# Down projection of an encoder layer: another way to form one set of weight sums, a later residual bias, spread convolution taps and another order of the last rows

## The chip, the cores and the metric

The kernel runs on one core of a Trainium2 chip. The metric is the device time of one execution in microseconds (us); the time before is a median of three runs. Beside the times there is one profiled execution, whose trace gives every duration used here. In the trace TensorE is PE (its weight loads PEld), VectorE is DVE, ScalarE is ACT, GpSimd is POOL and SyncE is SP.

## The reference, cut to what matters

One encoder layer on x of 1024 positions by 1024 channels: LayerNorm, a Fourier mixer, LayerNorm, a gated MLP with a depthwise convolution over positions, LayerNorm. All of it is float32.

```
h = layer_norm(DEEPNORM_ALPHA * h + mix, ln_tok_g, ln_tok_b)
u = depthwise_conv(h @ w_up, conv_w, conv_b)       # 2 x 2816 channels, 3 taps
g, v = split(u, 2)
ffn = (silu(g) * v) @ w_down                        # 2816 -> 1024
out = layer_norm(DEEPNORM_ALPHA * h + ffn, ln_ffn_g, ln_ffn_b)
```

The change touches the last stretch: the convolution of the last channel block, the down projection, the residual `ALPHA * h` and the last LayerNorm.

## The kernel before, in words

**Stages.** The mixer and the up projection run first (to 605 us of the span). The up projection goes by 22 channel blocks j of 128 channels; each block leaves a gate half and a value half of 128 channels by 1024 positions. `conv_taps(j, v, part)` starts the convolution of one half with an ACT operation and adds its taps on DVE (line 1086): parts 0 and 1 are two taps of 512 elements, parts 2 and 3 two taps of about 510 and two of one element. `conv_done(j)` applies Silu on ACT (L1120) and multiplies the halves on POOL (L1121); `store(j)` writes the product to the HBM scratch `gd` from ACT's DMA queue.

**Down projection.** It is a 2 by 2 block product done with seven instead of eight sub-products (a Strassen scheme), s = 0 to 6. Each sub-product multiplies a sum of quarters of the activations `g(k, h)` with a sum of quarters of the weights `w(k, h)`, and is 2816/2 channels deep: NK = 11 blocks of 128, taken two at a time as b = 0 to 5 (b = 5 has one). A pair (s, b) is called a block below. Float32 precision comes from splitting each operand into a high and a low part (`split`: ACT writes the high part, L184, DVE the low part, L181), and three matmuls for each product (`mm3`: L190 low x high, L192 high x low, L194 high x high). A full block has 24 matmuls of 512 columns on four PSUM banks `dn`; s = 6 is done row block by row block in the banks `dl`, at the very end.

**How operands are formed.** Three resident sets of tiles are used again and again: `sst[b]` (trace name sa), `tst[b]` (sb), and tiles fetched for one use (qa of activations, qw of weights). A sum is formed by an accumulating DMA from POOL's queue (`pile`, L1135): it adds a quarter from HBM (or from SBUF) onto a tile in place. A minus sign is made by `negate` on ACT (L1138) before the pile. In product 1 the activations are g(0,1) + g(1,1) and the weights w(0,1) - w(0,0): tst is negated and w(0,1) is piled on. Product 3 shows the other way: w(0,0) is fetched into a tile, and DVE subtracts (L1197). Product 2 negates sst and tst again and piles g(0,0) and w(1,1).

**The order of the work.** PE, DVE, ACT and POOL execute in the order in which the program is written, SP's fetches too. In the main loop, n counts the blocks: before block n's matmuls the program issues `down_load` for blocks up to n+5, `down_pile` up to n+4 and `down_prep` (the split) up to n+2. After the matmuls comes `extra(s, b)` with the other work: the last convolution, the loading of the eight accumulators `acc[i]` (the normed h, 128 rows by 1024), their scaling to ALPHA * h (`residual2`: one multiplication by `tokg`, L1220, and one addition of `tokb`, L1221, both on DVE, for each row block and each half), and `down_out(s)`, which adds the banks of a finished product to the accumulators (L1345). Buffers come from one pool of 46 tiles of 4 KB per partition; a fetch or a split waits until the tile whose place it takes has been read for the last time.

**The end.** After block (5, 5) DVE adds the last banks to rows 4 to 7 (L1424), takes the mean and variance (bn_stats, L1365; bn_aggr, L1369), POOL computes the reciprocal root (L223), DVE scales in two steps (L1305, L1314), and SP writes out. Rows 0 to 3 follow as the banks `dl` of product 6 become ready (L1435, L1436). Rows 0 to 3 get the bn_stats of their upper half early, in `extra(5, 2)`. The last row, 3, is written in three pieces: two on DVE, and one on ACT (L1311) and POOL (L1312).

Of the kernel before, what the change touches and what calls it, by code (L numbers as in the profile page):

```python
# [12 lines left out]
AF = mybir.ActivationFunctionType  # L13
ALU = mybir.AluOpType
# [8 lines left out]
NF = DFF // P  # L23
# [129 lines left out]
def encoder_layer(ctx: ExitStack, tc: tile.TileContext, a, out: bass.AP):  # L153
    nc = tc.nc
# [7 lines left out]
    def t4(shape, dt, name):  # L162
        return pool.tile(shape, dt, name=name, tag="t4", bufs=N4)
# [32 lines left out]
    hs = (slice(0, 512), slice(512, 1024))  # L196
# [515 lines left out]
    for bi in range(5):  # L712
        dft_cos(bi)
        if bi < 4:
            j, lst, i = later.pop(0)
            fold_split(j, lst, folds[j][i])
    for j in range(4):
        dft_sin(j)
        if later:
            k, lst, i = later.pop(0)  # L720
# [376 lines left out]
    def store(j):  # L1097
        k, b, kk = j // NK, j % NK // 2, j % NK % 2
        t = spill.pop(j)
        for h in range(2):  # L1100
            nc.scalar.dma_start(out=gd[k, h, b, :, kk], in_=t[:, hs[h]])

    def conv_taps(j, v, part=range(4)):
        c = cc[j][v]
        if 0 in part:
            ct[j, v] = t4([P, SEQ], F32, f"t{j}{v}")
        t = ct[j, v]
        w0 = 32 + 8 * j + 4 * v
        w = cols[:, w0 : w0 + 4]
        if 0 in part:  # L1110
            nc.scalar.activation(out=t, in_=c, func=AF.Identity, scale=w[:, 1:2], bias=w[:, 3:4])  # L1111
        taps = ((1, 513, -1, 0),), ((0, 512, 1, 2),), ((513, 1023, 1, 0),)
        taps += (((514, 1024, -1, 2), (512, 513, 511, 2), (1023, 1024, -511, 0)),)
        for i in part:
            for q in taps[i]:
                tap(t, c, w, *q)

    def conv_done(j):
        tg, tv = ct.pop((j, 0)), ct.pop((j, 1))
        nc.scalar.activation(out=tg, in_=tg, func=AF.Silu)  # L1120
        nc.gpsimd.tensor_tensor(out=tg, in0=tg, in1=tv, op=ALU.mult)  # L1121
        spill[j] = tg
# [6 lines left out]
    def fetch(name, src, b):  # L1129
        t = t4([P, 2, 512], F32, name)  # L1130
        nc.sync.dma_start(out=t[:, 0 : span(b)], in_=src)
        return t

    def pile(t, src):
        nc.gpsimd.dma_start(out=t[:, 0 : src.shape[1]], in_=src, accum_op=ALU.add)  # L1135

    def negate(t, b):
        nc.scalar.mul(t[:, 0 : span(b)], t[:, 0 : span(b)], -1.0)  # L1138
# [12 lines left out]
    def early(b):  # L1151
        sst[b] = fetch(f"sa{b}", quads_of(b)[0](0, 1), b)

    def down_load(s, b):
        g, w = quads_of(b)
        if s == 0:
            tst[b] = fetch(f"sb{b}", w(0, 0), b)
            dsrc[s, b] = fetch(f"qa{s}{b}", g(0, 0), b), tst[b]
        elif s == 1:
            dsrc[s, b] = sst[b], tst[b]  # L1160
        elif s == 2:
            dsrc[s, b] = sst[b], tst[b]
        elif s == 3:
            dsrc[s, b] = fetch(f"qa{s}{b}", g(1, 1), b), fetch(f"qw{s}{b}", w(0, 0), b)
        elif s == 4:
            dsrc[s, b] = sst[b], fetch(f"qw{s}{b}", w(1, 1), b)
        elif s == 5:
            dsrc[s, b] = fetch(f"qa{s}{b}", g(1, 1), b), tst[b]
        else:
            dsrc[s, b] = fetch(f"qa{s}{b}", g(1, 0), b), fetch(f"qw{s}{b}", w(1, 0), b)  # L1170

    def down_pile(s, b):
        g, w = quads_of(b)
        n = span(b)
        xa, xb = dsrc[s, b]
        if s == 1:
            negate(xb, b)
            pile(xa, g(1, 1))
            pile(xb, w(0, 1))
        elif s == 2:  # L1180
            negate(xa, b)
            negate(xb, b)
            pile(xa, g(0, 0))
            pile(xb, w(1, 1))
        elif s == 3:
            pile(xa, sst[b][:, 0:n])
        elif s == 4:
            pile(xa, g(1, 0))
        elif s == 5:
            negate(xb, b)  # L1190
            pile(xb, w(1, 0))

    def down_prep(s, b):
        n = span(b)
        xa, xb = dsrc.pop((s, b))
        if s == 3:
            nc.vector.tensor_tensor(out=xb[:, 0:n], in0=tst[b][:, 0:n], in1=xb[:, 0:n], op=ALU.subtract)  # L1197
        g = [t4([P, 2, 2, 256], F32R, f"ga{s}{b}{l}") for l in range(2)]
        w = [t4([P, 2, 512], F32R, f"wb{s}{b}{l}") for l in range(2)]
        split(g[0][:, 0:n], g[1][:, 0:n], xa[:, 0:n].rearrange("p k (j u) -> p k u j", u=2))  # L1200
        hi, lo = [x[:, 0:n] for x in w]
        if s == 2:
            nc.scalar.mul(hi, xb[:, 0:n], -1.0)  # L1203
            nc.vector.scalar_tensor_tensor(
                out=lo, in0=xb[:, 0:n], scalar=-1.0, in1=raw(hi), op0=ALU.mult, op1=ALU.subtract
            )
        else:
            split(hi, lo, xb[:, 0:n])
        dops[s, b] = g, w

    acc = []

    def load_acc(i):
        z = t4([P, D], F32, f"acc{i}")
        nc.sync.dma_start(out=z, in_=h1d[i])
        acc.append(z)

    def residual2(i, h):
        z = acc[i][:, hs[h]]
        nc.vector.tensor_tensor(out=z, in0=z, in1=tokg[:, hs[h]], op=ALU.mult)  # L1220
        nc.vector.tensor_tensor(out=z, in0=z, in1=tokb[:, hs[h]], op=ALU.add)  # L1221

    held = {1: 3, 2: 1}
    for j in range(NF):
        if j + 2 < NF:
# [22 lines left out]
        if j == NF - 1:  # L1248
            tokg, tokb = row(3, "tokg"), row(4, "tokb")
# [51 lines left out]
    def finish(i):  # L1301
        mv, rs = fin.pop(i)
        rc = slice(i * P, (i + 1) * P)
        z = acc[i]
        nc.vector.scalar_tensor_tensor(  # L1305
            out=z, in0=z, scalar=mv[:, 0, 0:1], in1=ffg, op0=ALU.subtract, op1=ALU.mult
        )
        pieces = (slice(0, 1024),) if i != 3 else (slice(0, 400), slice(400, 800))
        if i == 3:
            d = slice(800, 1024)  # L1310
            nc.scalar.activation(out=z[:, d], in_=z[:, d], func=AF.Identity, scale=rs)  # L1311
            nc.gpsimd.tensor_tensor(out=z[:, d], in0=z[:, d], in1=ffb[:, d], op=ALU.add)  # L1312
        for e in pieces:
            nc.vector.scalar_tensor_tensor(  # L1314
                out=z[:, e], in0=z[:, e], scalar=rs, in1=ffb[:, e], op0=ALU.mult, op1=ALU.add
            )
            nc.sync.dma_start(out=out[rc, e], in_=z[:, e])
        if i == 3:
            nc.scalar.dma_start(out=out[rc, d], in_=z[:, d])

    order = [(s, b) for s in range(7) for b in range(NB)]
    banks = {}
# [39 lines left out]
    def half_stats(i, h, parts=1):  # L1362
        if i not in s6:
            s6[i] = st([P, 1 + (2 if i == 3 else 1), 6], F32, f"obs{i}")
        nc.vector.bn_stats(out=s6[i][:, h], in_=acc[i][:, hs[h]])  # L1365

    def last_row(i):
        mv = st([P, 1, 2], F32, f"omv{i}")
        nc.vector.bn_aggr(out=mv[:, 0], in_=s6[i])  # L1369
        fin[i] = mv, rstd(mv, f"o{i}")  # L1370
        finish(i)

    def extra(s, b):
        if s == 0:
            if b == 0:
                store(NF - 2)
                for i in range(4):
                    load_acc(i)
                conv_taps(NF - 1, 1)
            elif b == 1:  # L1380
                conv_done(NF - 1)
                for i in range(4, 8):
                    load_acc(i)
            elif b == 2:
                store(NF - 1)
            for i in ((), (), (0,), (1,), (2,), (3,))[b]:
                residual2(i, 0)
        elif s == 1:
            if b == 0:
                down_out(0)  # L1390
            else:
                for i in ((0, 1), (2, 3), (4, 5), (6,), (7,))[b - 1]:
                    residual2(i, 1 if i < 4 else 0)
        elif b == 0:
            down_out(s - 1)
        elif s == 2 and b < 5:
            residual2(3 + b, 1)
        if s == 5 and b == 2:
            for i in range(4):
                half_stats(i, 1)  # L1400
            for i in range(4, 8):
                half_stats(i, 1)

# [5 lines left out]
    for n, (s, b) in enumerate(order[: 6 * NB]):  # L1409
# [10 lines left out]
        if (s, b) == (4, 0):  # L1420
            ffg, ffb = row(5, "ffg"), row(6, "ffb")
    for rb in range(4):
        z = acc[4 + rb][:, hs[0]]
        nc.vector.tensor_tensor(out=z, in0=z, in1=banks[1][rb], op=ALU.add)  # L1424
        half_stats(4 + rb, 0)
    for rb in range(4):
        last_row(4 + rb)
    for rb in range(4):
        pieces = (slice(0, 512),) if rb < 3 else (slice(0, 256), slice(256, 512))
        for pi, c in enumerate(pieces):  # L1430
            bk = bank(f"dl{rb}{pi}")
            for b in range(NB):
                down_mm(6, b, (rb,), {rb: bk[:, 0 : c.stop - c.start]}, c, b == 0, b == NB - 1)
            z = acc[rb][:, c]
            nc.vector.tensor_tensor(out=z, in0=z, in1=bk[:, 0 : c.stop - c.start], op=ALU.add)  # L1435
            nc.vector.bn_stats(out=s6[rb][:, 0 if pi == 0 else 2], in_=z)  # L1436
        last_row(rb)


# [18 lines left out]
```

## Time and profile before

| | |
|---|---|
| median of three runs | 838.26 us (837.71 to 842.68) |
| profiled execution | 839.37 us |
| its span | 837.6 us |
| PE busy | 807.7 us (96%) |
| DVE busy | 688.7 us (82%) |
| ACT busy | 388.4 us (46%) |
| POOL busy | 269.9 us (32%) |
| DMA queue of accumulating transfers (q0) | 30.23 MB, 18.7% of 16 engines' span |
| DMA queue of SP's fetches (q1) | 80.51 MB, 27.4% |

The profiled execution lies 1.77 us above its own span and 1.11 us above the median. A timeline row gives start, duration, engine, line, operation and out<-in, and in brackets the idle time before it and what ended that. A row of windows gives for a stretch its length and then, for each engine, busy time and the count of instructions, the granted clock of TensorE (PEclk), the busy share of the DMA engines and what they moved. Neighbouring instructions of an engine overlap a little, so what one more costs is the distance between starts.

### The profile page before, as it was taken

Reading aid. Unit: us, or ns where it says so; the run is one execution under the profiler, and the core shown is the slowest. Engines: PE = TensorE matmul, PEld = TensorE weight load, DVE = VectorE, ACT = ScalarE, POOL = GpSimd, SP = SyncE. Lnnn points to the kernel's source line nnn. Section 1 sums busy time; section 2 is a strip of 40 time slices with the busy share of each in tenths; the row PEclk is TensorE's granted clock in tenths of the full one; section 3 lists DMA queues with packets and bytes.
Section 4 is the critical chain, followed back from the end, with each engine's and each line's share of the span. In section 5 each row is a group of like instructions: output and inputs, shape, how many; then the busy total and the mean of one; then the engine's idle time right before and its main releaser. Section 6 shows DMA issues by size and latency. Waiting matters only on the chain.

```text
span 837.6 us, 10455 instructions
## 1 busy us (share of the span) xinstructions
PE 807.7 (96%) x3816; PEld 665.1 (79%) x3816; DVE 688.7 (82%) x1005; ACT 388.4 (46%) x595; POOL 269.9 (32%) x204
## 2 busy tenths in 40 slices
PE   8899999988899999999999999999999999999995
PEld 6899978776688888888888888888878877888885
DVE  4996778988988998887888888888796968974887
ACT  4545714864544443344444344344564744573400
POOL 3333012122053454444444444444042320220032
PEclk9999999999999999999999999999999999999999
DMA  9876544534122222222322222223889999998122
GB/s 338 286 135 142 172 120 141 139 98 127 51 101 76 76 76 75 76 79 94 101 101 79 76 76 76 75 76 114 303 303 232 223 275 280 250 291 269 71 101 101
DMA packets 40138, 123.07 MB, mean 147 GB/s; under 512 B 4566, under 2 KB 5462, under 8 KB 40086
## 3 DMA queue, kind: packets, MB, share of 16 engines
q1 hardware_dynamic: 23830, 80.51, 27.4%
q0 software_dynamic: 9776, 30.23, 18.7%
q10 hardware_dynamic: 6480, 11.65, 3.7%
q8 instruction: 30, 0.49, 0.2%
q14 instruction: 22, 0.18, 0.1%
HBM read 98.52 MB, written 19.92 MB: 141 GB/s over the span
## 4 chain that ended last, share of the span: by engine, by line
PE 68%; DVE 12%; issue 8%; DMA 5%; POOL 4%; ACT 2%; SPq 1%; DVEq 0%; POOLq 0%; ACTq 0%
PE by L190 7%; PE by L194 7%; PE by L192 7%; PE bz L190 5%; PE bz L194 5%; PE bz L192 5%; PE dn L192 4%; PE dn L190 4%; PE dn L194 4%; PE bx L190 4%; PE bx L192 4%; PE bx L194 4%; DMA sb<-wd 2%; POOL sa L1135 1%; DVE acc L1314 1%
## 5 line engine op out<-in xcount | busy, mean ns | idle before, releaser
L1086 DVE SCALAR_TENSOR_TENSOR t<-c,cols,t 128x1 f32<-128x1 f32 (+2 forms) x264 | 141.9, 586 | 3.4 <-ACT t L1111 0.2
L1121 POOL TENSOR_TENSOR t<-t,t 128x1024 f32<-128x1024 f32 x22 | 54.6, 2481 | 245.1 <-DVE t L1086 177.0
L190 PE MATMUL by<-b,a 128*128 128x512 f32 (+1 forms) x268 | 105.6, 394 | 5.5 <-DVE a L181 5.5
L192 PE MATMUL dn<-wb,ga 128*128 128x512 f32 x264 | 105.3, 399 | 3.3 <-DVE wb L181 1.8
L190 PE MATMUL dn<-wb,ga 128*128 128x512 f32 x264 | 105.6, 400 | 0.9 <-ACT wb L1203 0.9
L194 PE MATMUL by<-b,a 128*128 128x512 f32 (+1 forms) x268 | 105.2, 393 | 0.0
L192 PE MATMUL by<-b,a 128*128 128x512 f32 (+1 forms) x268 | 105.0, 392 | 0.0
L194 PE MATMUL dn<-wb,ga 128*128 128x512 f32 x264 | 104.9, 397 | 0.0
L181 DVE TENSOR_TENSOR a<-s,a 128x512 fp32r<-128x512 f32 x88 | 86.6, 986 | 15.2 <-ACT a L900 15.0
L190 PE MATMUL bx<-b,a 128*128 128x512 f32 (+1 forms) x192 | 72.8, 379 | 1.8 <-DVE a L181 1.8
L192 PE MATMUL bx<-b,a 128*128 128x512 f32 (+1 forms) x192 | 72.2, 376 | 0.0
L194 PE MATMUL bx<-b,a 128*128 128x512 f32 (+1 forms) x192 | 72.1, 376 | 0.0
L190 PE MATMUL bz<-b,a 128*128 128x512 f32 (+1 forms) x180 | 70.5, 391 | 1.6 <-DVE a L181 1.6
L192 PE MATMUL bz<-b,a 128*128 128x512 f32 (+1 forms) x180 | 70.0, 389 | 1.5 <-DVE b L181 1.5
L194 PE MATMUL bz<-b,a 128*128 128x512 f32 (+1 forms) x180 | 70.2, 390 | 0.0
L181 DVE TENSOR_TENSOR a<-wr,a 128x512 fp32r<-128x512 f32 x66 | 68.8, 1045 | 0.6 <-ACT a L900 0.6
L190 PEld LDWEIGHTS by<-b,a 128*128 128x128 f32 x268 | 50.8, 189 | 18.2 <-DVE a L181 6.5
L192 PEld LDWEIGHTS dn<-wb,ga 128*128 128x128 f32 x264 | 50.4, 191 | 16.3 <-DVE wb L181 2.6
L949 DVE TENSOR_TENSOR c<-bz,c 128x512 f32<-128x512 f32 x44 | 30.4, 691 | 38.7 <-PE bz L194 38.0
L190 PEld LDWEIGHTS dn<-wb,ga 128*128 128x128 f32 x264 | 50.2, 190 | 13.3 <-ACT wb L1203 1.8
L1272 ACT COPY c<-bx 128x512 f32<-128x512 f32 x22 | 12.9, 587 | 103.1 <-DVE c L949 103.1
L194 PEld LDWEIGHTS by<-b,a 128*128 128x128 f32 x268 | 50.7, 189 | 11.5
(338 smaller groups left out, 1808.5 us busy)
## 6 DMA issues: line engine op xcount, KB each, us to landing
wr<-wup SPq DMA_DIRECT2D x44, 512.0 KB
gd<-t ACTq DMA_DIRECT2D x44, 256.0 KB
qa<-gd SPq DMA_DIRECT2D x20, 512.0 KB
sa<-gd POOLq DMA_DIRECT2D x15, 512.0 KB, 14.6
sb<-wd POOLq DMA_DIRECT2D x15, 512.0 KB, 12.0
qw<-wd SPq DMA_DIRECT2D x15, 512.0 KB
x<-x SPq DMA_DIRECT2D x8, 512.0 KB
acc<-h1d SPq DMA_DIRECT2D x8, 512.0 KB
```

Source lines behind the costliest of these rows:

```text
L181: eng.tensor_tensor(out=lo, in0=src, in1=raw(hi), op=ALU.subtract)
L190: nc.tensor.matmul(outs[i], ll, rh[i], start=first, stop=False, **kw)
L192: nc.tensor.matmul(outs[i], lh, rl[i], start=False, stop=False, **kw)
L194: nc.tensor.matmul(outs[i], lh, rh[i], start=False, stop=last, **kw)
L949: nc.vector.tensor_tensor(out=o, in0=b, in1=x, op=ALU.add)
L1086: nc.vector.scalar_tensor_tensor(out=t[:, lo:hi], in0=c[:, lo + sh : hi + sh], scalar=w[:, wi : wi + 1], in1=t[:, lo:hi], op0=ALU.mult, op ...
L1121: nc.gpsimd.tensor_tensor(out=tg, in0=tg, in1=tv, op=ALU.mult)
L1135: nc.gpsimd.dma_start(out=t[:, 0 : src.shape[1]], in_=src, accum_op=ALU.add)
L1272: nc.scalar.copy(out=cg[:, 0:512], in_=bx[j])
L1314: nc.vector.scalar_tensor_tensor(out=z[:, e], in0=z[:, e], scalar=rs, in1=ffb[:, e], op0=ALU.mult, op1=ALU.add)
```

## The change

1. **Weights of product 1.** w(0,1) is fetched by SP into a tile of its own (`tq`, trace name qw, issued in `down_load` like the others), and DVE forms w(0,1) - w(0,0) in place in tst (new L1202). ACT's negation and POOL's accumulating DMA for this set go: six of each, five full and one half.
2. **Residual bias.** `residual2` only multiplies. `add_bias` adds `tokb` to each accumulator by an accumulating DMA out of SBUF (new L1156), rows 4 to 7 after block (4, 1), rows 0 to 3 after block (5, 1).
3. **Last block's taps.** The four parts of `conv_taps(21, 1)` are split between block (0, 0) and block (0, 1); `conv_done(21)` and `store(21)` follow one block later than before.
4. **End.** The bn_stats of rows 0 to 3's upper half move from block (5, 2) into the last rows; row 2 is finished after the first piece of row 3; row 3 is written in two pieces of 640 and 384 columns, both by DVE.

```diff
+    def add_bias(rows):
+        for i in rows:
+            nc.gpsimd.dma_start(out=acc[i], in_=tokb, accum_op=ALU.add)
+    tq = {}
     def down_load(s, b):
...
         elif s == 1:
+            tq[b] = fetch(f"qw{s}{b}", w(0, 1), b)
             dsrc[s, b] = sst[b], tst[b]
...
         if s == 1:
-            negate(xb, b)
             pile(xa, g(1, 1))
-            pile(xb, w(0, 1))
...
-        if s == 3:
+        if s == 1:
+            nc.vector.tensor_tensor(out=xb[:, 0:n], in0=tq.pop(b)[:, 0:n], in1=xb[:, 0:n], op=ALU.subtract)
+        elif s == 3:
...
         nc.vector.tensor_tensor(out=z, in0=z, in1=tokg[:, hs[h]], op=ALU.mult)
-        nc.vector.tensor_tensor(out=z, in0=z, in1=tokb[:, hs[h]], op=ALU.add)
...
-        pieces = (slice(0, 1024),) if i != 3 else (slice(0, 400), slice(400, 800))
-        if i == 3:
-            d = slice(800, 1024)
-            nc.scalar.activation(out=z[:, d], in_=z[:, d], func=AF.Identity, scale=rs)
-            nc.gpsimd.tensor_tensor(out=z[:, d], in0=z[:, d], in1=ffb[:, d], op=ALU.add)
-        for e in pieces:
+        for e in (slice(0, 1024),) if i != 3 else (slice(0, 640), slice(640, 1024)):
...
-                conv_taps(NF - 1, 1)
+                conv_taps(NF - 1, 1, (0, 1))
             elif b == 1:
-                conv_done(NF - 1)
                 for i in range(4, 8):
                     load_acc(i)
+                conv_taps(NF - 1, 1, (2, 3))
             elif b == 2:
+                conv_done(NF - 1)
+            elif b == 3:
                 store(NF - 1)
...
-        if s == 5 and b == 2:
-            for i in range(4):
-                half_stats(i, 1)
+        if (s, b) == (4, 1):
+            add_bias(range(4, 8))
+        elif (s, b) == (5, 1):
+            add_bias(range(4))
+        elif (s, b) == (5, 2):
             for i in range(4, 8):
                 half_stats(i, 1)
...
     for rb in range(4):
+        half_stats(rb, 1)
...
+            if rb == 3 and pi == 0:
+                last_row(2)
+        if rb != 2:
+            last_row(rb)
```

On DVE, at the first blocks of product 0, the difference reads as follows. t_5280 is the value half of the last channel block, ga and wb are the low parts of a block's operands: those with qa_5226 and sb_5224 belong to block (0, 3), those with qa_5230 and sb_5228 to (0, 4).

```order
 L1086 SCALAR_TENSOR_TENSOR t_5280<-c_5038,cols,t_5280 128x512 x2
+L181 TENSOR_TENSOR ga_5287<-qa_5226,ga_5286 128x1024
+L181 TENSOR_TENSOR wb_5289<-sb_5224,wb_5288 128x1024
 L1086 SCALAR_TENSOR_TENSOR t_5280<-c_5038,cols,t_5280 128x510 x2
 L1086 SCALAR_TENSOR_TENSOR t_5280<-c_5038,cols,t_5280 128x1 x2
-L181 TENSOR_TENSOR ga_5289<-qa_5226,ga_5288 128x1024
-L181 TENSOR_TENSOR wb_5291<-sb_5224,wb_5290 128x1024
 L181 TENSOR_TENSOR ga_5336<-qa_5230,ga_5335 128x1024
```

The low parts of block (0, 3) now stand behind two of the taps, not behind all of them.

On POOL, where the up projection ends, these rows stood before. L1121 is the product of the two halves (t_5212 is that of the last channel block), sa the activations and sb the weights of product 1.

```order
L1121 TENSOR_TENSOR t_5098<-t_5098,t_5202 128x1024
L1121 TENSOR_TENSOR t_5212<-t_5212,t_5280 128x1024
L1135 DMA sa_5244<-gd 128x1024
L1135 DMA sb_4981<-wd 128x1024
L1135 DMA sa_5296<-gd 128x1024
L1135 DMA sb_5106<-wd 128x1024
L1135 DMA sa_5343<-gd 128x1024
```

And these stand there now:

```order
L1121 TENSOR_TENSOR t_5098<-t_5098,t_5202 128x1024
L1135 DMA sa_5244<-gd 128x1024
L1121 TENSOR_TENSOR t_5212<-t_5212,t_5280 128x1024
L1135 DMA sa_5294<-gd 128x1024
L1135 DMA sa_5343<-gd 128x1024
L1135 DMA sa_5383<-gd 128x1024
L1135 DMA sa_5424<-gd 128x1024
L1135 DMA sa_5463<-gd 128x512
```

The first pile of product 1 moved ahead of the last product of halves, and the piles of weights are gone from between the others.

On POOL, between the piles of products 4 (sa) and 5 (sb), before:

```order
L1135 DMA sa_5384<-gd 128x1024
L1135 DMA sa_5423<-gd 128x1024
L1135 DMA sa_5462<-gd 128x512
L1135 DMA sb_4981<-wd 128x1024
L1135 DMA sb_5106<-wd 128x1024
```

And now:

```order
L1135 DMA sa_5424<-gd 128x1024
L1135 DMA sa_5463<-gd 128x512
L1156 DMA acc_5320<-tokb 128x1024
L1156 DMA acc_5322<-tokb 128x1024
L1156 DMA acc_5324<-tokb 128x1024
L1156 DMA acc_5326<-tokb 128x1024
L1135 DMA sb_4981<-wd 128x1024
L1135 DMA sb_5106<-wd 128x1024
```

The four bias transfers of rows 4 to 7 stand ahead of all piles of product 5; those of rows 0 to 3 stand behind them.

More of the change, by code (lines that the diff above doesn't have):

```diff
@@ L1317, in finish @@
             nc.sync.dma_start(out=out[rc, e], in_=z[:, e])
-        if i == 3:
-            nc.scalar.dma_start(out=out[rc, d], in_=z[:, d])
     order = [(s, b) for s in range(7) for b in range(NB)]
@@ L1436, in encoder_layer @@
             nc.vector.bn_stats(out=s6[rb][:, 0 if pi == 0 else 2], in_=z)
-        last_row(rb)
+            if rb == 3 and pi == 0:
+                last_row(2)
+        if rb != 2:
+            last_row(rb)
 def kernel(**inputs):
```

## The prediction

> **What bounds the kernel now.** I read the page first, then the windows of the `dn` matmuls block by block, then what ended PE's pauses, the chain of waits behind the longest, and the tail.
>
> ```profile
> PE 807.7 (96%) x3816; PEld 665.1 (79%) x3816; DVE 688.7 (82%) x1005; ACT 388.4 (46%) x595; POOL 269.9 (32%) x204
> ```
>
> PE is the bound. The change starts at 606 us, so only three things can move: the pace of product blocks, their pauses, and the tail. Windows from the first matmul of a block to that of the next (length, PE, PEld, DVE, PEclk, DMA share, GB/s), blocks (0,2), (0,3), (2,2), (2,3), (2,4), (3,2), then all of product 5:
>
> ```profile
> 617.07:622.96 5.89, 5.87 (x25) 4.44 (x24) 0.00 (x0) 1.00 0.82 277
> 622.96:632.10 9.14, 7.39 (x25) 5.60 (x24) 0.00 (x0) 0.81 1.04 330
> 682.12:688.01 5.89, 5.73 (x26) 4.33 (x24) 4.31 (x8) 1.00 1.05 274
> 688.01:695.62 7.61, 6.11 (x24) 4.42 (x24) 0.00 (x0) 1.00 1.07 279
> 695.62:703.88 8.26, 7.49 (x25) 5.77 (x25) 0.00 (x0) 0.79 1.08 213
> 717.75:723.28 5.53, 5.53 (x25) 4.50 (x24) 0.00 (x0) 1.00 1.07 237
> 767.59:798.02 30.43, 30.43 (x133) 24.61 (x131) 2.10 (x4) 1.00 0.29 102
> ```
>
> An undisturbed block takes 5.53 us, a product 30.43. Two places lose time. Gap 1, block (0,3): 9.14 - 5.53 = 3.61. Gap 2, blocks (2,2) to (2,4): 21.76 - 16.59 = 5.17. Together 8.78. Block (0,2) loses 0.36 in addition; what it waits for is not touched.
>
> Gap 1, in the timeline:
>
> ```profile
> 615.96 1.06 ACT L184 CAST wb<-sb 128x1024 fp32r<-128x1024 f32 x1
> 617.35 3.24 DVE L1086 SCALAR_TENSOR_TENSOR t<-c,cols,t 128x512 f32<-128x512 f32 x6
> 620.51 1.22 DVE L181 TENSOR_TENSOR ga<-qa,ga 128x1024 fp32r<-128x1024 f32 x1
> 620.81 3.16 POOL L1121 TENSOR_TENSOR t<-t,t 128x1024 f32<-128x1024 f32 x1 [7.91 <-ACT ga L184]
> 621.64 3.41 DVE L181 TENSOR_TENSOR wb<-sb,wb 128x1024 fp32r<-128x1024 f32 x1
> 625.11 0.50 PE L192 MATMUL dn<-wb,ga 128*128 128x512 f32 x1 [1.75 <-DVE wb L181]
> 626.15 0.63 PE L192 MATMUL dn<-wb,ga 128*128 128x512 f32 x1
> ```
>
> ACT has written the high parts of (0,3) by 617.0, but DVE first does six tap operations. Its second subtraction takes 3.41 instead of 1.22 us: it ends just after POOL's product, which runs beside it. PE waits 1.75 us and then issues slowly (0.63 each, PEclk 0.81 over the block); that stretch is the other half of the loss.
>
> Gap 2, in the chain of waits:
>
> ```profile
> 674.00 20.43 DMA sb<-wd
> 694.51 1.07 ACT wb L1203
> 695.60 1.24 DVE wb L1204
> 696.88 0.50 PE dn L192
> ```
>
> The weights of block (2,4) were in the DMA queue for 20.43 us. What filled it (MB and share of 16 engines, first 637 to 659 us, then 660 to 700):
>
> ```profile
> q0 software_dynamic: 1414, 4.61, 107.1%
> ...
> q0 software_dynamic: 1837, 6.15, 77.9%
> q1 hardware_dynamic: 1152, 4.19, 27.9%
> ```
>
> In the first window accumulating transfers alone fill the engines: 22 us x 0.524 / 4.61 MB = 2.50 us for each 512 KB. In the second, 40 us x 27.9 / 105.8 for eight fetches (4.19 MB) makes 1.32 us for a fetch. An accumulating transfer costs the engines almost two fetches.
>
> **The change, part by part.**
>
> *Taps.* Only the two 512-element taps, about half of the 3.24 us, now stand before the low parts of (0,3): DVE reaches them at 617.35 + 1.45 = 618.8 and is done at 618.8 + 2 x 1.13 (their distance, 621.64 - 620.51) = 621.1, 1.9 us before PE needs them at 622.96. POOL's product now meets block (0,4): the other taps end at about 622.8, the first subtraction starts then, the second waits for POOL until 626.1 and ends at 627.3. PE starts (0,4) at 617.07 + 5.89 + 5.53 = 628.5. Gap 1 goes: -3.6. If this cover of 1.2 us failed, the same pause would return one block later, so the bounds are -3.6 and 0.
>
> *Weights of product 1.*
>
> ```profile
> L1197 DVE TENSOR_TENSOR qw<-sb,qw 128x1024 f32<-128x1024 f32 x5 | 6.1, 1219 | 0.0
> L1221 DVE TENSOR_TENSOR acc<-acc,tokb 128x512 f32<-128x512 f32 x16 | 11.1, 692 | 0.6
> L1138 ACT ACTIVATE sb<-sb 128x1024 f32<-128x1024 f32 x15 | 15.8, 1055 | 4.0 <-POOL t L1121 4.0
> 654.82 0.87 POOL L1135 DMA_DIRECT2D sb<-wd  x1
> ```
>
> ACT loses five and a half negations of 1.06, POOL as many issues of 0.87, the engines 5.5 x (2.50 - 1.32) = 6.5 us. DVE gains 5.5 x 1.22 = 6.7 us and loses the sixteen bias additions, 11.1 us; both lie under PE. The six more fetches go through SP past the loads of `acc` and of sa; they need tiles that the last taps free, at 623 to 626 us, where before sa's fetches waited for the same. DVE now waits for qw of block (1,b) with the later blocks behind it; block (1,0) begins about 637, a product after the start.
>
> Does gap 2 go? Block (2,4)'s weights arrive at 694.4 and are usable at 696.9. Without its own pause in (2,3) PE would want them at 682.12 + 11.06 = 693.2, and with gap 1 gone at 689.6: they must come 7.3 us earlier. The queue ran without a break from 624 on. It now starts product 1 with two fetches and one pile done before POOL's product, and has 6.5 us less to do; its piles for product 2, issued from 654 while product 1's drained, would find an empty queue from about 648, where ACT and DVE have split (1,3). From there ten piles and eight fetches are 25 + 10.6 = 35.6 us: 683.6, so 10.8 us earlier. That is 3.5 us better than needed. Gap 2 goes: -5.2; bounds -5.2 and 0, and I take the full value with less trust than for gap 1.
>
> At both places half the loss is the slow clock after the wait. [...]
>
> *Bias.* Eight accumulating transfers, 8 x 2.50 = 20 us of the engines. Those of rows 0 to 3 fall where the engines are idle (0.29 in product 5). Those of rows 4 to 7 wait for product 3's banks and stand ahead of product 5's piles:
>
> ```profile
> 735.28 2.78 DVE L1345 TENSOR_TENSOR acc<-acc,dn 128x512 f32<-128x512 f32 x4 [1.30 <-PE dn L194]
> 735.20 0.87 POOL L1135 DMA_DIRECT2D sb<-wd  x1 [14.53 <-ACT sb L1138]
> 745.83 1.23 DVE L181 TENSOR_TENSOR wb<-sb,wb 128x1024 fp32r<-128x1024 f32 x1 [0.22 <-ACT wb L184]
> ```
>
> All of this 8.8 us earlier: the bias goes out from 729, the first pile of product 5 at about 732.8 instead of 726.4, with four transfers ahead of it. At 2.5 us each it lands at 729 + 5 x 2.5 = 741.5; PE wants block (5,0) at 767.59 - 8.8 = 758.8, less 2.3 for ACT and DVE 756.5. Cost: nothing, up to 27.5 / 5 = 5.5 us a transfer; the bound above is in the rivals.
>
> *End.*
>
> ```profile
> 796.15 0.69 DVE L1424 TENSOR_TENSOR acc<-acc,dn 128x512 f32<-128x512 f32 x1 [3.23 <-PE dn L194]
> 796.87 0.69 DVE L1365 BATCH_NORM_STATS2 obs<-acc 128x6 f32<-128x512 f32 x1
> 797.48 0.67 DVE L1424 TENSOR_TENSOR acc<-acc,dn 128x512 f32<-128x512 f32 x1
> 827.19 1.28 DVE L1314 SCALAR_TENSOR_TENSOR acc<-acc,o2rs,ffb 128x1024 f32<-128x1024 f32 x1 [0.45 <-POOL o2rs L223]
> 828.39 0.41 DVE L1435 TENSOR_TENSOR acc<-acc,dl 128x256 f32<-128x256 f32 x1
> 828.84 0.43 DVE L1436 BATCH_NORM_STATS2 obs<-acc 128x6 f32<-128x256 f32 x1
> 832.14 1.64 DVE L1314 SCALAR_TENSOR_TENSOR acc<-acc,o3rs,ffb 128x400 f32<-128x400 f32 x2 [0.44 <-POOL o3rs L223]
> 832.70 0.66 POOL L1312 TENSOR_TENSOR acc<-acc,ffb 128x224 f32<-128x224 f32 x1 [0.59 <-ACT acc L1311]
> L194 PE MATMUL dl<-wb,ga x55: 277/391/399, 798.5 to 828.6; 128*128 128x512 f32 x33, 128*128 128x256 f32 x22
> ```
>
> From 796.15 DVE is one chain, broken only by the 0.44 us before POOL's root; PE is done with row 3's first piece before DVE takes it. So every DVE operation here counts. Four more bn_stats, 797.48 - 796.87 = 0.61 each: +2.4. The last scaling loses its meeting with POOL's L1312 and does 1024 columns instead of 800: from 1.64 to about 1.4 us (an estimate: row 2's 1.28 for 1024 columns in one piece, and a second start): -0.2. Putting row 2 behind row 3's first piece moves work within the same chain and saves about 0.1. End: +2.1 (bounds +1.4, if POOL's earlier finish shortens the 3.8 us after DVE's last row, and +2.7).
>
> *Sum.* -3.6 - 5.2 + 2.1 = -6.7. Span 837.6 - 6.7 = 830.9, the profiled execution 832.7; on the median 838.26 - 6.7 = **831.6 us**.
>
> **Rivals.**
>
> *One gap stays.* If gap 1 only moves to (0,4): 838.26 - 5.2 + 2.1 = 835.2. If gap 2 stays, because the 3.5 us are eaten by tile waits of the extra fetches or late negations: 838.26 - 3.6 + 2.1 = 836.8. For it speaks the DMA share above 1.04 in every window of product 2; against it the 6.5 us freed. [...] The rows say 2.50 against 1.32.
>
> [...]
>
> *Slower: the bias holds up product 5.* At 7 us a transfer the first pile lands at 764, block (5,0) is usable at 766.3 instead of 758.8 (7.5 lost, 1.6 of slow clock as in gap 1), and five more blocks come at 7 instead of 5.53 (+6.6): 831.6 + 15.7 = 847.3. It decides above 5.5 us. The nearest rows give 2.5 alone and, beside fetches, 40 x 0.524 / 6.15 = 3.4; four additions from SBUF in a row, beside fetches, are not in the trace.
>
> **Numbers.** Forecast (both gaps close) 0.58; gap 1 stays 0.09; gap 2 stays 0.15; only idle time 0.04; slower 0.14, in which I count any pause of this size that I have not seen. A measurement here tells about 1% from no change, 8.4 us. The forecast's 6.7 lies under it; the runs before spread by 5 us, so a fifth of the forecast's chance passes that bound: faster 0.12, slower 0.14, same 0.74. Range: from 829 (end at its lower bound, all 0.36 of (0,2) too) to 838, which takes in the cases of one gap: about 0.8.
>
> **What would show it.** Right: blocks (0,3) and (2,2) to (2,4) at 5.53, PEclk 1.00 in all windows from 606, the wait for L1204 gone, product 5 starting near 758.8, DVE's tail about 39.7 us long instead of 37.6. Wrong: a PE pause before (0,4), in product 2, or at (5,0) with L1156 transfers in the queue; DVE's tail shorter than before.

## The result and the profile after

The changed kernel took 846.08 us (median of 6 runs, 845.36 to 847.69), the kernel before in all its 6 runs on that chip 838.78 us (836.77 to 842.68): ratio 1.0086, 95% interval 1.0061 to 1.0111. The change makes it slower by 0.9%, 7.3 us; 831.6 was forecast. One of the ten executions of a later kernel, that with taps and weights alone, took 1608.37 us: its median counts it, its ratio does not. The profiled execution took 847.69 us, its span is 845.9. In the page of the changed kernel the first line, that of the engines, shows the same number of matmuls as before:

```profile
PE 808.5 (96%) x3816; PEld 666.8 (79%) x3816; DVE 682.9 (81%) x995; ACT 382.3 (45%) x588; POOL 269.6 (32%) x205
```

The windows of the changed kernel for the same blocks as in the prediction, (0,2), (0,3), (2,2), (2,3), (2,4), (3,2), and product 5 (length, PE, PEld, DVE, ACT, POOL, PEclk, DMA share, GB/s):

```profile
619.57:625.43 5.86, 5.84 (x26) 4.43 (x25) 5.79 (x10) 4.15 (x6) 0.00 (x0) 1.00 0.97 333
625.43:631.02 5.59, 5.59 (x25) 4.52 (x24) 5.59 (x5) 1.13 (x1) 3.98 (x2) 1.00 0.94 334
680.81:686.37 5.56, 5.56 (x26) 4.50 (x24) 5.24 (x9) 2.19 (x2) 2.93 (x4) 1.00 1.06 275
686.37:693.69 7.32, 6.00 (x25) 4.24 (x24) 2.76 (x4) 2.18 (x2) 0.79 (x1) 1.00 1.06 279
693.69:700.43 6.74, 5.98 (x24) 4.61 (x25) 5.39 (x7) 2.92 (x4) 0.08 (x1) 1.00 1.09 214
714.21:719.74 5.53, 5.53 (x26) 4.50 (x24) 5.49 (x7) 2.23 (x3) 2.29 (x3) 1.00 1.07 221
764.13:794.70 30.57, 30.57 (x134) 24.79 (x133) 17.56 (x20) 15.17 (x16) 4.43 (x6) 1.00 1.00 275
```

Block (0,3) now takes 5.59 instead of 9.14: gap 1 is gone, and no pause came before (0,4). Gap 2 is 1.79 + 1.21 = 3.0 instead of 5.17: smaller, not gone. No wait came ahead of (5,0). PE leaves product 5 at 794.70, 3.3 us earlier than before, though product 0 began 2.5 us later (608.44 against 605.94; where that comes from is told with the second profile of the kernel before). The end, though, comes 8.3 us later. The last row shows where to look: the DMA share of product 5 is 1.00, where it was 0.29. DVE in the timeline of that stretch:

```profile
777.17 2.47 DVE L1363 BATCH_NORM_STATS2 obs<-acc 128x6 f32<-128x512 f32 x4
779.55 1.21 DVE L181 TENSOR_TENSOR ga<-qa,ga 128x1024 fp32r<-128x1024 f32 x1
791.31 1.23 DVE L181 TENSOR_TENSOR wb<-qw,wb 128x1024 fp32r<-128x1024 f32 x1 [10.54 <-DMA acc<-tokb]
...
802.14 0.68 DVE L181 TENSOR_TENSOR wb<-qw,wb 128x512 fp32r<-128x512 f32 x1
802.74 0.68 DVE L1426 TENSOR_TENSOR acc<-acc,dn 128x512 f32<-128x512 f32 x1
...
840.95 1.41 DVE L1314 SCALAR_TENSOR_TENSOR acc<-acc,o3rs,ffb 128x640 f32<-128x640 f32 x2 [0.44 <-POOL o3rs L223]
```

DVE stands still for 10.54 us ahead of an operation that has nothing to do with the bias: the low weights of block (6,0). Behind it on DVE wait all other low parts of product 6, and behind these the tail. The tail's first operation (L1426, in the kernel before L1424) starts at 802.74. Before, it started 0.91 us after the first matmul of (5,5) (796.15 against 795.24); here that matmul is at 791.93, so the tail was due at 792.84 and is 802.74 - 792.84 = 9.9 us late. From there to the end of DVE it lasts 39.6 us (802.74 to 842.36), before 37.6.

What that operation waits for is seen in the list of semaphores of the built program (wb601 is that low part; DMASW are POOL's transfers, DMAHW a fetch). First before the change, then after:

```
L181 TENSOR_TENSOR wb601_6509<-qw60_6398,wb600_6508 128x1024 [waits DMAHW0_49,Activation_49]
L181 TENSOR_TENSOR wb601_6499<-qw60_6392,wb600_6498 128x1024 [waits DMASW6_49,DMASW7_49,DMASW5_49,DMAHW6_49,DMASW4_49,Activation_49]
```

It reads neither `acc` nor `tokb`. It writes a tile, and `tokb` is one of the 46 tiles of the pool too (`row` takes it from `t4`). The last reader of `tokb` is now the last bias transfer, and the tile that takes its place is this one: in the built program of the changed kernel both have the same address (131776 in each partition); in that of the kernel before their addresses differ.

POOL's rows and the DMA view of the changed kernel from 769.2 to 790.8 us show the transfers:

```profile
732.72 3.54 POOL L1156 DMA_DIRECT2D acc<-tokb  x4 [13.69 <-DVE acc L1343]
769.19 3.54 POOL L1156 DMA_DIRECT2D acc<-tokb  x4 [0.46 <-DVE acc L1343]
```

```profile
q0 software_dynamic: 831, 2.75, 64.3%
q1 hardware_dynamic: 909, 3.31, 40.8%
...
acc<-tokb POOLq DMA_DIRECT2D x4, 512.0 KB, 15.2
```

For the engines a bias transfer costs 21.6 us x 0.643 x 0.524 / 2.75 = 2.65 us, a fetch beside it 21.6 x 0.408 x 0.524 / 3.31 = 1.40 us. In the packets' records the two queues start about as many packets each: in the thirteen stretches of 1.5 us from 769.5 to 789.0 us 48 to 78 of q0 and 50 to 77 of q1, never more than 6 apart within a stretch. The four transfers of rows 0 to 3 land 3.81 us apart, the last at 790.75, and the fetches of product 6 between them land 3.81 us apart too.

### The profile page after: what moved, and what is told of

Its sections match the earlier page's. It is cut to its first block, busy times and chain, and to the rows that moved or that the text cites. A ratio compares the mean times of both kernels' runs of the same rounds, so it can differ in the third digit from the quotient of the medians.

```text
span 845.9 us, 10455 instructions
## 1 busy us (share of the span) xinstructions
PE 808.5 (96%) x3816; PEld 666.8 (79%) x3816; DVE 682.9 (81%) x995; ACT 382.3 (45%) x588; POOL 269.6 (32%) x205
## 5 line engine op out<-in xcount | busy, mean ns | idle before, releaser
L1121 POOL TENSOR_TENSOR t<-t,t 128x1024 f32<-128x1024 f32 x22 | 54.2, 2463 | 249.6 <-DVE t L1086 197.1
L190 PE MATMUL by<-b,a 128*128 128x512 f32 (+1 forms) x268 | 107.1, 400 | 5.5 <-DVE a L181 5.5
L194 PE MATMUL by<-b,a 128*128 128x512 f32 (+1 forms) x268 | 106.2, 396 | 0.0
L192 PE MATMUL by<-b,a 128*128 128x512 f32 (+1 forms) x268 | 106.1, 396 | 0.0
L192 PE MATMUL dn<-wb,ga 128*128 128x512 f32 x264 | 104.2, 395 | 1.4 <-DVE wb L1211 1.3
L190 PE MATMUL dn<-wb,ga 128*128 128x512 f32 x264 | 103.9, 394 | 0.7 <-ACT wb L1210 0.7
L194 PE MATMUL dn<-wb,ga 128*128 128x512 f32 x264 | 103.7, 393 | 0.0
L190 PEld LDWEIGHTS by<-b,a 128*128 128x128 f32 x268 | 51.6, 192 | 18.0 <-DVE a L181 6.5
L194 PEld LDWEIGHTS by<-b,a 128*128 128x128 f32 x268 | 51.6, 192 | 11.8
L192 PEld LDWEIGHTS by<-b,a 128*128 128x128 f32 x268 | 51.7, 193 | 11.5
```

Of the source, the lines that this page charges most:

```text
L190: nc.tensor.matmul(outs[i], ll, rh[i], start=first, stop=False, **kw)
L192: nc.tensor.matmul(outs[i], lh, rl[i], start=False, stop=False, **kw)
L194: nc.tensor.matmul(outs[i], lh, rh[i], start=False, stop=last, **kw)
```

## Experiments: what holds up the tail

Theory A: the place of `tokb`. Theory B: the engines that the bias takes from the fetches of product 6. Theory C: the tail itself grew.

**A place of its own.** The added lines, with two transfers for each row block; the old `tokb` is still loaded, and nobody reads it late:

```diff
+            t = t2([P, 512], F32, f"bias{h}")
+            nc.sync.dma_start(out=t, in_=a["rows"][4][:, hs[h]].broadcast_to([P, 512]))
...
-            nc.gpsimd.dma_start(out=acc[i], in_=tokb, accum_op=ALU.add)
+            for h in range(2):
+                nc.gpsimd.dma_start(out=acc[i][:, hs[h]], in_=bias[h], accum_op=ALU.add)
```

> The changed kernel, but the transfers add the bias from two tiles of 512 columns that belong to no place of the 46 (two transfers of 256 KB for each row block instead of one of 512 KB); tokb itself is still loaded and scaled, but nobody reads it. Theory A (place): the low weights of block (6,0) wait 10.54 us, from 780.8 to 791.3, because they take the place of tokb, which the last bias transfer reads until 790.75. Then that wait is gone here; DVE still gets the last operands of product 6 late, because their fetches share the engines with the bias (the last lands at 794.25), so its first tail operation starts about 796.5 instead of 802.74: 846.1 - 6.2 = 840 us. Theory B (engines): the transfers cost time only by what they take from the fetches; then the DVE tail starts about 802 as before and the time stays at 846. Theory C: DVE's idle time there costs nothing and the tail itself is what grew; also 846.

Measured: 841.53 us, before 837.86; ratio 1.0066 (1.0038 to 1.0094). DVE in its timeline:

```profile
776.67 1.21 DVE L181 TENSOR_TENSOR ga<-qa,ga 128x1024 fp32r<-128x1024 f32 x1
777.80 1.22 DVE L181 TENSOR_TENSOR wb<-qw,wb 128x1024 fp32r<-128x1024 f32 x1
...
793.86 1.22 DVE L181 TENSOR_TENSOR wb<-qw,wb 128x1024 fp32r<-128x1024 f32 x1 [1.41 <-ACT wb L184]
...
796.21 0.68 DVE L1440 TENSOR_TENSOR acc<-acc,dn 128x512 f32<-128x512 f32 x1
```

The wait of 10.54 us is gone: theory A for that wait, and C falls. But now DVE waits block by block for operands whose fetches come late, as expected (five waits of 0.94 to 1.44 us), and the tail still starts at 796.21, 5.7 us after product 5 would let it (its (5,5) begins at 789.62). Of the 9.9 us the place explains 4.2 by this run, the shared engines 5.7. The run does not change the place alone: each transfer is also cut in two, so the split is good to what that costs, which no run shows.

**Rows 0 to 3 by DVE, as before the change.**

```diff
         nc.vector.tensor_tensor(out=z, in0=z, in1=tokg[:, hs[h]], op=ALU.mult)
+        if i < 4:
+            nc.vector.tensor_tensor(out=z, in0=z, in1=tokb[:, hs[h]], op=ALU.add)
...
-        elif (s, b) == (5, 1):
-            add_bias(range(4))
```

> The changed kernel, but the bias of rows 0 to 3 is added by DVE right after its multiplication, as before the change; only rows 4 to 7 get it by transfers. The last reader of tokb is then done at about 753. Theory A (place) and theory B (engines): both the wait and the late fetches go, DVE's tail starts at the end of product 5 as it did before (about 793 on the profile's scale, 9.9 us earlier): 836.2 us. Together with the run with a place of its own this splits the two: A alone gives about 840 there, B alone 846 there. Theory C (the tail grew by its own work): 846 here.

Measured: 837.76 us, before 837.86; ratio 1.0012 (0.9997 to 1.0028). The tail starts when PE is done:

```profile
792.89 0.69 DVE L1427 TENSOR_TENSOR acc<-acc,dn 128x512 f32<-128x512 f32 x1 [3.20 <-PE dn L194]
```

The loss is gone, and it came from the four transfers of rows 0 to 3 alone; those of rows 4 to 7 are still there. SP issued its last fetch for product 6 at 775.87, in the changed kernel at 776.06: the fetches were not sent late there, they landed late, as theory B has it. The time is 1.6 us above what was expected; in this profile gap 2 was 1.2 us larger (0.92 + 2.08 + 1.20). So with this loss gone the other parts of the change together bring nothing that the times show.

**All eight ahead of product 5.** This tests the prediction's slower rival at double dose.

```diff
-            add_bias(range(4, 8))
-        elif (s, b) == (5, 1):
-            add_bias(range(4))
+            add_bias((4, 5, 6, 7, 0, 1, 2, 3))
```

> The changed kernel, but all eight bias transfers go out after block (4,1), ahead of all piles of product 5. It tests the mechanism of the slower rival of the prediction at double dose. A bias transfer beside a fetch took 3.81 us in the changed kernel (742.12, 745.92, 749.73, 753.54), and the first pile of product 5 landed at 757.04, 4.8 us ahead of the need (764.13 less 2.3 for ACT and DVE). Four more: 757.0 + 15.2 = 772.3, usable at 774.6, so PE pauses about 10.5 us ahead of block (5,0). The place of tokb comes free at about 769, before product 6 is prepared, so the 10.5 us wait of DVE goes: 846.1 - 9.9 + 10.5 = 846.7 us, some 1.5 more if a slow clock follows. If the transfers of rows 0 to 3 were cheap (2.5 us each, 10 in all), PE's pause would be 5.2 and the time 841.

Measured: 846.93 us, before 837.86; ratio 1.0124 (1.0099 to 1.0150). The windows of (4,5) and (5,0):

```profile
759.94:769.87 9.93, 2.94 (x14) 2.07 (x12) 0.02 (x1) 1.10 (x2) 0.00 (x0) 0.88 1.07 219
769.87:778.01 8.14, 7.67 (x25) 5.80 (x25) 6.82 (x7) 7.37 (x8) 2.60 (x3) 0.72 1.00 225
```

The first pile of product 5 landed at 768.41, and PE lost 7.16 in the window of (4,5), which holds the pause before (5,0), and 2.61 in (5,0), 9.8 in all. So the rival's mechanism exists; with four transfers it stays away, since the first pile then lands at 757.04, 4.8 us before it is needed (764.13 less 2.3).

## Experiments: where the gain went

**Taps and product 1's weights alone** (bias and end as before):

> The kernel before with two parts of the change alone: the last taps spread, and product 1's weights by fetch and DVE. Bias and tail as before. Theory D (gate by ACT): gap 1 closes (-3.6) and gap 2 shrinks as in the changed kernel from 5.15 to about 3.0, since the first piles of product 2 still wait for ACT's negations, which stand behind the splits of product 1: 838.8 - 3.6 - 2.1 = 833.1 us. The prediction's theory (both gaps close by the freed time of the engines): 830.0 us. If gap 2 only absorbs what gap 1 gives back: 838.8 us.

Measured: 837.82 us, before 837.86; ratio 1.0005 (0.9983 to 1.0028). No gain, 4.7 us above the expectation. In the profile the down projection did get shorter, from the first matmul to the last landing 224.6 us against 229.4 in the profile before, with gap 2 at 0.25 + 2.08 + 1.19 and 0.37 in (3,0). Two things stood against it: product 0 began late here too (608.95), and the end: from DVE's last operation to the end of the span 5.7 us passed, before 3.8. The next runs took these apart.

**The kernel before, profiled again.**

> The kernel before, unchanged, profiled a second time. In its first profile product 0 began at 605.94; in the profiles of five kernels of this study, whose program is the same up to there, at 606.88 to 608.95. The difference arises after one pause of PE near 211 us: it is equally long in all of them, but the up projection ran at the slow pace behind it in those five and not in that profile; and behind gap 2 it was the reverse. Theory E (the slow stretch behind a pause comes or stays away from run to run): here the stretch near 214 us can be there, product 0 then begins at 607.5 to 609, and gap 1 and gap 2 can come without their slow stretches: gap 1 1.8 to 3.6, gap 2 3.5 to 5.2. Theory F (it belongs to the kernel): product 0 at 605.9, gap 1 at 3.6 and gap 2 at 5.15 again.

Measured: 839.36 us. Windows, first of the start of the up projection in the first profile of the kernel before:

```profile
210.00:222.00 12.00, 9.07 (x40) 7.08 (x39) 11.28 (x20) 5.43 (x8) 0.11 (x1) 1.00 0.00 0
```

and in the second, with its blocks (0,3), (2,3) and (2,4):

```profile
210.00:222.00 12.00, 9.07 (x29) 6.85 (x28) 11.29 (x20) 5.41 (x8) 0.00 (x0) 0.72 0.00 0
625.24:632.80 7.56, 5.81 (x25) 4.43 (x24) 7.49 (x9) 3.10 (x4) 7.17 (x8) 1.00 1.04 283
688.38:695.67 7.29, 6.01 (x26) 4.25 (x24) 3.44 (x5) 2.17 (x2) 0.68 (x2) 1.00 1.07 282
695.67:703.92 8.25, 7.49 (x24) 5.74 (x25) 7.90 (x10) 4.07 (x5) 0.34 (x1) 0.79 1.08 214
```

Theory E holds. After the same pause (PE's longest wait there is 2.9 us in both) PE started 40 matmuls in the one profile and 29 in the other, at a clock of 1.00 and 0.72; product 0 begins at 608.22. And gap 1 comes here without its slow stretch, after the same pause of 1.75 us: 2.03 instead of 3.61. At these two places, then, the slow stretch comes in one execution and not in another of the same program. Gap 1 is worth about 2 us and a chance of 1.6 more, gap 2 here 1.76 + 2.72 = 4.5. From the first matmul to the last landing this profile takes 227.1 us, so of the 4.8 us by which taps and weights seemed shorter 2.3 were chance.

**Taps alone.**

> The kernel before with the taps of the last block spread, nothing else. Both theories of gap 1 agree that DVE then reaches the low parts of block (0,3) in time and block (0,3) takes about 5.55. Theory G (absorbed): the weights of (2,3) and (2,4) come when ACT's negations and the transfer queue let them, so PE, which is 1.8 to 3.6 us earlier, waits longer in gap 2: gap 2 5 to 7 us of idle time, median 837 to 838.5. The prediction's rival for gap 2 staying as it was (both parts add): 838 - 3.6 = 834.

Measured: 837.75 us, before 838.05; ratio 0.9994 (0.9975 to 1.0013). Block (0,3) is undisturbed, gap 2 is 0.87 + 2.08 + 1.16 = 4.1. Theory G is right in the time, but not in its size: gap 2 did not take 5 to 7, so gap 2 did not absorb what gap 1 gave back. Products 0 to 5 took 187.7 us in this profile and 189.8 in the second of the kernel before. The 2 us are not to be seen in the median, whose interval just allows 2.1; why not stays open.

**Product 1's weights alone.**

> The kernel before with product 1's weights by fetch and DVE, nothing else. Gap 1 stays (DVE still behind six taps and POOL's product): 1.8 to 3.6. Theory D (product 2's piles start when ACT has negated, not when the engines are free): gap 2 as in the changed kernel or a little smaller, 2 to 3 us instead of 5.15, median 835.5 to 837. The prediction's theory (the freed 6.5 us go to gap 2 in full): gap 2 closes, block windows of product 2 all 5.55, median 833.

Measured: 841.19 us, before 838.05; ratio 1.0032 (1.0014 to 1.0050): slower, which no theory expected. Gap 2 is as large as before (0.80 + 2.08 + 1.15, and 0.44 in (3,0), against 4.5). Most of the loss is at the end, in POOL's closing drain, the instruction with which POOL closes the program. These are the records of POOL's instructions in the trace, in us:

| kernel | accumulating transfers | POOL's last operation ends | drain ends | between |
|---|---|---|---|---|
| before | 70 | 833.35 | 836.79 | 3.44 |
| taps alone | 70 | 829.97 | 833.40 | 3.43 |
| weights alone | 64 | 834.24 | 839.55 | 5.31 |
| taps and weights | 64 | 831.60 | 836.91 | 5.31 |
| rows 0 to 3 by DVE | 68 | 831.09 | 834.35 | 3.26 |
| changed kernel | 72 | 840.91 | 844.51 | 3.60 |
| a place of its own | 80 | 834.37 | 838.62 | 4.25 |

With the six transfers gone the drain is 1.87 us longer, and the end of these two programs comes 0.7 to 0.8 us behind it, at 840.3 and 837.7 (before the change too, at 837.6: POOL's drain ends at 836.79, SP's at 836.00). Against the second profile of the kernel before, weights alone lost 2.7 us of span: 0.5 by a later start of product 0, 0.4 in products 0 to 5, 1.9 in the drain. Taps and weights together started 0.7 later, gained 2.5 in products 0 to 5 and lost 1.9 in the drain: the two spans are the same within 0.1 us.

**Taps, weights, and product 2's operands formed one block earlier.** In the changed kernel the DMA engines stood nearly idle when the first transfer of product 2 could have gone out; the DMA view from 638 to 655 us (tenths of the 16 engines), and the rows of ACT and POOL:

```profile
DMA  9999999999989999999999999999982119989200
```

```profile
650.49 1.12 ACT L184 CAST ga<-sa 128x1024 fp32r<-128x1024 f32 x1 [4.38 <-PE dn L194]
651.52 1.05 ACT L184 CAST wb<-sb 128x1024 fp32r<-128x1024 f32 x1
652.47 1.05 ACT L1138 ACTIVATE sa<-sa 128x1024 f32<-128x1024 f32 x1
```

```profile
653.82 0.86 POOL L1135 DMA_DIRECT2D sa<-gd  x1 [2.48 <-ACT sa L1138]
```

ACT waits 4.38 us for a place that PE must leave, then splits (1,3), and only then negates for product 2. The edit issues these steps one block earlier (and the last pile of product 1 with them), so that the negation goes first:

```diff
+            if step is down_pile and 2 * NB - 1 <= done[step] < 3 * NB:
+                lead += 1
```

> The kernel with taps and weights alone, in which the steps that form product 2's operands are issued one block earlier: ACT negates (2,0) ahead of the split of (1,3) instead of behind it, and POOL's transfers follow at once. Theory D: in the changed kernel the engines stood nearly idle around 652 us and the first transfer of product 2 went out only at 653.82, when ACT came to the negations. Here it goes out 4 to 6 us earlier, the weights of (2,3) and (2,4) land 3 to 5 us earlier against PE, and gap 2 (2.08 + 1.18 + 0.25 in the run without this) falls below 1: 837.8 - 3 = 834.8. If the transfers themselves are the limit (the queue is then merely longer): gap 2 stays and the time is 837.8.

Measured: 834.55 us, before 838.05; ratio 0.9955 (0.9935 to 0.9974). ACT negates at 646.08, and the stretch that holds gap 2 is without a pause:

```profile
646.08 1.06 ACT L1138 ACTIVATE sa<-sa 128x1024 f32<-128x1024 f32 x1
```

```profile
681.00:700.00 19.00, 19.00 (x83) 15.40 (x82) 13.11 (x16) 6.01 (x7) 1.72 (x2) 1.00 1.06 279
```

The first transfer of product 2 goes out at 650.33 instead of 653.44 in the run without this edit, 3.1 us earlier where 4 to 6 were expected; the weights of (2,4) land at 687.92 instead of 693.51, by the semaphores' records. Theory D holds: gap 2 closes, and the freed engine time is used.

**The earlier step alone.**

> The kernel before, in which only the steps that form product 2's operands are issued one block earlier; taps and product 1's weights as before. Theory H (freed engines and an earlier issue are worth something only together): before the change the transfers of product 1 filled the queue until about 661, so product 2's transfers, issued 4 to 6 us earlier, wait behind them; the weights of (2,4) land at about 694 as before and gap 2 stays at 4 to 5: 838. Rival (the earlier issue alone is what closed gap 2 in the run with it): gap 2 below 1.5, 838 - 3 = 835.

Measured: 839.10 us, before 838.77; ratio 1.0004 (0.9985 to 1.0024); gap 2 is 1.61 + 2.71. Here the first transfer of product 2 goes out at 648.82 (653.87 in the first profile of the kernel before), but the transfers of product 1 ahead of it land until 658.71, and the weights of (2,4) land at 693.15. Theory H holds. Freed engines alone bring next to nothing here, as ACT comes to its negations no sooner (weights alone: gap 2 is 4.5 as before; in the changed kernel at 652.47, before at 652.52); an earlier issue alone brings next to nothing, as the transfers of product 1 still fill the queue until 658.71 (gap 2 is 4.3); both together, in the run that also has the taps, close the gap.

**With row 3 on DVE alone,** as in the changed kernel (`slice(0, 640), slice(640, 1024)`, without ACT and POOL):

> The kernel with taps, weights and the earlier issue, and from the changed kernel the two pieces of row 3 on DVE (640 and 384), so that ACT and POOL no longer take part in row 3; the order of the rows and the early bn_stats as before. POOL's closing drain took 5.31 us behind its last operation in the three kernels with 64 accumulating transfers, 3.44 with 70, 3.26 with 68, 4.25 with 80; the program's end waits for it. POOL's last operation is now the root of row 3, 1.3 us earlier: the end comes with the drain at about -1.3: 834.55 - 1.3 = 833.3 us. If the end followed DVE alone (0.2 us shorter): 834.3. If it followed the landing of the last output (DVE's end and 3.5 us): 832.2.

Measured: 832.54 us, before 838.77; ratio 0.9927 (0.9907 to 0.9947). POOL's drain takes 5.31 us again, begins earlier and still ends last (828.75; SP's ends at 827.55). From the first matmul of product 6 to the end of the span 40.14 us pass, 41.40 without this edit: -1.26, as expected. **And with the bias of rows 4 to 7 by transfers** (64 become 68):

> The same, and the bias of rows 4 to 7 by the transfers of the change (rows 0 to 3 on DVE), so 68 accumulating transfers instead of 64. DVE's place waits do not appear, since the last reader of tokb is done near 750; product 5's first pile stays 4 to 5 us ahead of its need, since issue and need both moved. If the closing drain of POOL goes with the count as in the other runs, it takes 3.26 instead of 5.31 us, and the end follows the last output: 832.2 us, 1.1 below the run without. If the drain does not go with it: 833.3, as without.

Measured: 831.07 us, before 838.77; ratio 0.9916 (0.9896 to 0.9936), the best of the study. The drain takes 3.27 us (825.85 to 829.12), as in the other kernel with 68. The two intervals overlap, so that these four transfers gain something is not settled by the times; in the profiles product 6 and the end take 38.99 us instead of 40.14, 1.15 less, as expected, and SP's last output now ends last (829.97). Left out of the change are only the late bias and bn_stats of rows 0 to 3 and the place of row 2.

## Why the prediction was wrong

**Bias, rows 0 to 3: the step that failed.** "Those of rows 0 to 3 fall where the engines are idle (0.29 in product 5)" set their cost at nothing. The cover named was the wrong one: the idle engines. With the fetches of product 6 the transfers kept the engines busy for some 22 us of that stretch, and the fetches came late (5.7 us). And the transfers kept `tokb` in use until 790.75, so that a low part of product 6 waited for its place with the rest of DVE's program behind it (4.2 us more). Together it cost 9.9 us. The prediction asked whether the engines are free, and not which fetches follow in that stretch, nor who inherits the tile that is read.

**Bias, rows 4 to 7: right.** Nothing lost at (5,0). The price was 3.8 us a transfer instead of 2.5, with fetches running between them; the named bound of 5.5 was not reached, and in the run with eight transfers ahead of product 5 PE lost 9.8 us there.

**Slower rival: right side, wrong place.** It priced the bias against product 5's piles (847.3 us). What came (846.1) was the bias against product 6 and DVE. Its chance of 0.14, "in which I count any pause of this size that I have not seen", was too small: the change had four unseen transfers in two places, and only one was worked out.

**Taps: right in kind, mis-sized.** The pause went and nothing came before (0,4). The -3.6 holds 1.6 of a slow stretch that came in one profile of the kernel before and not in the other; about -2.0 belongs to the gap.

**Weights of product 1: the second step that failed.** Freed engine time was there, but of the 6.5 us only a part lay idle at that place: the engines' busy shares of the six microseconds from 650 to 656 add up to 3.45, so some 2.5 us were idle. And "from about 648, where ACT and DVE have split (1,3)" did not come true: the first transfer of product 2 went out at 653.82, before at 653.87, since ACT came to its negation no sooner (652.47, before 652.52). Gap 2 went from 4.5 (second profile) to 3.0, -1.5 instead of -5.2.

**End: right.** +2.0 on DVE's chain (39.6 against 37.6) and -0.2 behind it, +2.1 was predicted. That POOL's finish could shorten the end was in its bounds; how much the drain changes with the number of transfers (3.26 to 5.31 us) was not.

**The sum** against the second profile of the kernel before, which has the same span of 837.6: start +0.2, the blocks up to (5,5) -3.6 (gap 1 -2.0, gap 2 -1.5), late tail +9.9, tail +2.0, behind it -0.2: +8.3, the 845.9 of the changed kernel. In the prediction's own range the lower end, 829, lies 1.5 us below what the terms named for it give (831.6 - 0.7 - 0.36 = 830.5).

**The slow clock and the price of a transfer.** The length of a pause did not settle here whether the slow clock follows it: one and the same pause before 222 us (PE's longest wait 2.9 us) ended at clock 1.00 in one profile and 0.72 in another, and that of 1.75 us in gap 1 at 0.81 and 1.00. What decides it no run shows. For the case that only idle time returns (0.04 in the prediction) no run shows a cause by which the clock would keep a slow stretch: with gap 1's pause gone block (0,3) takes 5.59 us at a clock of 1.00. It would still have been right about the half of gap 1, where about 2.0 us belong to the pause and 1.6 are chance. That an accumulating transfer costs the engines almost two fetches held: the window from 769.2 to 790.8 us shows 2.65 us for 512 KB of the one kind and 1.40 for 512 KB of the other, where the prediction had 2.50 and 1.32.

## What to carry to other kernels

When a read is moved later, ask which tile it keeps in use, which instruction takes that tile's place, and what stands behind that instruction on its engine: here four transfers put into idle time cost 9.9 us, 4.2 of them because DVE, which works in program order, waited 10.54 us for the place of their source. The freed engine time (6.5 us by the prediction's estimate) closed gap 2 here only when the next issuer could use it (3.5 us were left with taps and weights alone, none with the earlier step); look for the instruction that gates the issue, and move both. Of the 3.6 us that one profile showed for gap 1, 1.6 were chance: profile the old kernel twice before a gap is priced.

## What was not expected of the hardware

The slow stretch behind a pause of PE came in one profile of the kernel before and not in the other: in gap 1 in the first, where it cost 1.6 us, and behind the pause at 211 us in the second, where product 0 began 2.3 us later. Behind two pauses of 0.73 to 0.77 us at block (2,4) it came in some kernels (before the change, the earlier step alone: 8.2 to 8.3 us for the block) and not in others (the changed kernel, taps alone: 6.7). What decides it stays open.

POOL's closing drain took 3.26 us with 68 accumulating transfers, 3.44 with 70, 3.60 with 72 and 4.25 with 80, 0.08 to 0.09 for each, but 5.31 with 64, in each of four kernels. Why 64 stands apart stays open.
